# All low weight parts on VectorE, unscaled attention output, and diagonal blocks by the DMA's addressing, in a one-core hybrid encoder block

## The chip, the cores and the metric

The kernel runs on one core of one Trainium2 chip. A core has TensorE (PE, matmuls; its weight loads are shown apart as PEld), VectorE (DVE), ScalarE (ACT), GpSimd (POOL) and SyncE (SP, which here issues every DMA). Each engine works through its own instruction list in order; between engines there are only semaphores. The metric is the device time of one execution in microseconds. The kernel before takes 1120.7 us (median of 3 runs, 1119.09 to 1123.05).

## The reference

One layer of a streaming encoder for 512 tokens with 1024 features, in float32. Three sub-blocks follow each other, each with an RMS norm, a scale and a shift made from a conditioning vector, and a gated residual:

```
x = x + 0.5*g1 * swiglu(mod(x), ffn1)            # 1024 -> 2 x 2816 -> 1024
h = mod(x)
x = x + g2 * (concat(gated_delta_net(h), latent_attention(h)) @ w_out)
x = x + 0.5*g3 * swiglu(mod(x), ffn2)

# latent attention, per head of 4, per block of 128 queries
q_nope = rms(q_nope)*scale;  q_rope = rope(rms(q_rope))*scale
o_b = softmax(q k^T, chunk-causal) @ v
o_b = rms(o_b, mla_out_norm_w)                   # y * rsqrt(mean(y*y) + EPS)

# delta net, per head of 4: a triangular system per chunk of 64 tokens
M = I + strict_lower(beta * k k^T * decay);  W = solve(M, [beta*v, beta*exp(G)*k])
```

The norm after the softmax product is what the second part of the change uses: a row's scale cancels in it, up to the place of EPS.

## The kernel before

**Precision and weights.** Matmuls of float32 quality are made from three products of rounded parts (`mm3`, L261 to L263): high weight by high data, high by low, low by high. Each weight tile, a *unit* of 128 x 1024, is loaded by SP into `wr`; ACT casts it into the high part `wh` (L192), and the low part `wl = wr - wh` is one subtraction (L193). A switch `pool_lo` says which engine subtracts: VectorE in the two feed-forward blocks, GpSimd from the end of the first feed-forward block to the first units of the second one, that is in the mixer and the two norms around it. The tiles `wr`, `wh`, `wl` have four buffers each, so the load of a unit waits until the `wl` of the fourth unit before it is made, and its cast until PE has read the old one.

**The order of work.** A scheduler lays out each engine's list ahead of time from the program order and its own estimate of durations; the lists are then fixed. The program sets PE's order in some stretches (`matmuls_in_order`). The stages in the profiled time:

- 0 to about 380 us: modulation vectors and the first feed-forward block, mostly 128x512 matmuls.
- 380 to 430: the last output tiles of it, and `norm_half`: column sums of the squares `na` (L508), the row factor `ry` on GpSimd (L178), its diagonal `dg` (L428), a matmul that spreads it (L436) into `rb`, and then per feature tile `hm` (L454), `hh` (L456, ACT) and `hl` (L448), on which the next matmuls wait. It is done for each half of the tokens.
- 430 to about 500: latent projections (`latents`, `lifts`) and the first convolved tiles.
- 500 to 690: the dense units of the mixer are PE's filling, and between them run, as generators stepped in turn, `prep_q`, `prep_k`, `attend`, `delta_a`, `base_blocks`, `inverse`, `solve`.
- 690 to 760: the recurrence over 128-token blocks (`recur`, `gated_out`), the output projection (`out_half`, L1711) and the next `norm_half`.
- 760 to the end: the second feed-forward block.

**The places that the change touches.** `base_blocks` (L1172) inverts the 16x16 diagonal blocks of the triangular matrices `at`: it masks each `at` (L1182, four products on VectorE), folds the eight column groups by a reduction (L1184), writes the folded tile `bd` to DRAM and reads it back with a block on each partition (`ba`, L1186 and L1188), solves row by row on VectorE (L1200, L1201), and brings the result back in the same way (`t_d`, `t16`). `inverse` (L1211) starts from that result with four masked products per pair of chunks. `prep_q` (L1404) sums squares of queries by two reductions per tile, makes two row factors by integer start and three Newton steps (`rsqrt`, L173), and rotates the queries a block at a time (`rope`, L1490). `attend` (L1502) takes the row sum `l` of the exponentials, its reciprocal `li` on VectorE (L1519), and scales the product with it as it leaves PSUM (L1530, VectorE). `attended` (L1536) normalises the finished head. `z_done` in `mixer` (L1567) copies the gate projections out of PSUM on VectorE.

Of the kernel before, what the change touches and what calls it, by code (L numbers as in the profile page):

```python
# [77 lines left out]
class Block:  # L78
    def __init__(self, ctx, tc, ins, out):
# [111 lines left out]
    def split_w(self, raw, hi, lo):  # L191
        self.nc.scalar.copy(hi, raw)  # L192
        (self.nc.gpsimd if self.pool_lo else self.nc.vector).tensor_tensor(out=lo, in0=raw, in1=hi.bitcast(F32),  # L193
                                                                           op=ALU.subtract)
# [977 lines left out]
    def base_blocks(self):  # L1172

        nc, v = self.nc, self.nc.vector
        a_d = self.dp.tile([16, 8, 16, 16], F32, tag="a_d", name="a_d")
# [4 lines left out]
        m4 = self.dmask.unsqueeze(1).to_broadcast([P, 4, P])  # L1180
        for p in range(NB):
            m = self.slot(s="bm")  # L1182
            self.mul(m.rearrange("p (h c) -> p h c", h=4), self.at[p].rearrange("p (h c) -> p h c", h=4), m4)
            v.tensor_reduce(out=d[:, 64 * p:64 * p + 64].rearrange("p (h c) -> p h c", h=4),  # L1184
                            in_=m.rearrange("p (h i c) -> p h c i", h=4, i=8), axis=AX.X, op=ALU.add)
# [566 lines left out]
```

## Time and profile before

| | before |
|---|---|
| median of 3 runs | 1120.7 us |
| the profiled execution's own time | 1120.38 us |
| its span, first to last instruction | 1118.7 us |
| mean granted TensorE clock | 0.978 |
| PE busy | 1074.4 us, 96% |
| VectorE busy | 588.7 us, 53%, 1062 instructions |
| ACT busy | 376.4 us, 34%, 605 instructions |
| GpSimd busy | 132.6 us, 12%, 133 instructions |
| low weight parts on VectorE / on GpSimd | 133 / 37 |

Line numbers (L193) are those of the kernel before. Groups and waits carry the program's tile names, output first. The granted clock is a share of full speed: at 0.5 the same matmul takes twice the time, and PE is busy all the same, so a stage can lose time both as idle time of PE and as clock.

### The profile page before, as it was taken

To read this page: it belongs to the slowest core of one execution; us is meant where nothing else is said; L and a number is where in the kernel's file an instruction comes from. 1 tells how busy PE (TensorE), PEld (TensorE's weight loads), DVE (VectorE), ACT (ScalarE), POOL (GpSimd) and SP (SyncE) were. 2 spreads that over 40 slices of the span, in tenths; PEclk is the share of its full clock that TensorE was granted. 3 is DMA by queue.
4 is the path that set the end of the run, shared out by engine and by line. 5 is a ranking of instruction groups with operands and counts; after the bars stand their busy time and mean duration, and the time that the engine had idled before them with its cause. 6 is when DMAs were issued, how large, how long until landed. Compare 5 with 4: busy or idle time off the path is not lost. (4 is left out here: it accounts for less than half of the span.)

```text
span 1118.7 us, 14192 instructions
## 1 busy us (share of the span) xinstructions
PE 1074.4 (96%) x5591; PEld 891.8 (80%) x5591; DVE 588.7 (53%) x1062; ACT 376.4 (34%) x605; POOL 132.6 (12%) x133
## 2 busy tenths in 40 slices
PE   6999999999999979987999999979999999999998
PEld 5788788788887978966777768978888888888888
DVE  4489784333776266277777735875333333332220
ACT  4342322222222236464445244434232222222220
POOL 1000000000000245333122123440000000000000
PEclk8999999999999989998999989989999999999999
DMA  9989863333876363221112001123333333333420
GB/s 282 261 259 315 262 188 94 95 94 104 273 235 215 92 174 87 57 57 52 43 43 71 20 20 39 38 76 93 96 95 94 95 95 99 98 90 103 114 71 29
DMA packets 208625, 131.91 MB, mean 118 GB/s; under 512 B 11553, under 2 KB 192686, under 8 KB 208558
## 3 DMA queue, kind: packets, MB, share of 16 engines
q1 hardware_dynamic: 208558, 131.00, 39.6%
q8 instruction: 44, 0.72, 0.3%
q14 instruction: 23, 0.19, 0.1%
HBM read 128.63 MB, written 2.36 MB: 117 GB/s over the span
## 5 line engine op out<-in xcount | busy, mean ns | idle before, releaser
L261 PE MATMUL pa<-hh,wh 128*128 128x512 f32 (+1 forms) x885 | 341.5, 386 | 5.6 <-DVE xT L1711 2.4
L192 ACT CAST wh<-wr 128x1024 fp32r<-128x1024 f32 (+1 forms) x170 | 173.4, 1021 | 503.9 <-PE pa L262 322.6
L263 PE MATMUL pa<-hh,wl 128*128 128x512 f32 (+1 forms) x885 | 338.5, 382 | 0.0
L262 PE MATMUL pa<-hl,wh 128*128 128x512 f32 (+1 forms) x885 | 338.4, 382 | 0.1
L193 DVE TENSOR_TENSOR wl<-wr,wh 128x1024 fp32r<-128x1024 f32 (+1 forms) x133 | 156.6, 1178 | 208.5 <-ACT wh L192 199.9
L261 PEld LDWEIGHTS pa<-hh,wh 128*128 128x128 f32 x885 | 169.3, 191 | 40.7 <-issue 3.1
L263 PEld LDWEIGHTS pa<-hh,wl 128*128 128x128 f32 x885 | 169.1, 191 | 31.9 <-issue 0.5
L262 PEld LDWEIGHTS pa<-hl,wh 128*128 128x128 f32 x885 | 169.1, 191 | 30.7 <-issue 0.5
L261 PE MATMUL pa<-ah,wh 128*128 128x512 f32 (+1 forms) x418 | 150.1, 359 | 0.0
L263 PE MATMUL pa<-ah,wl 128*128 128x512 f32 (+1 forms) x418 | 148.8, 356 | 0.0
L262 PE MATMUL pa<-al,wh 128*128 128x512 f32 (+1 forms) x418 | 148.6, 356 | 0.0
L193 POOL TENSOR_TENSOR wl<-wr,wh 128x1024 fp32r<-128x1024 f32 (+1 forms) x37 | 89.5, 2426 | 274.8 <-ACT wh L192 243.7
L261 PEld LDWEIGHTS pa<-ah,wh 128*128 128x128 f32 x418 | 79.0, 189 | 12.7 <-ACT wh L192 1.7
L263 PEld LDWEIGHTS pa<-ah,wl 128*128 128x128 f32 x418 | 79.0, 189 | 11.3
L262 PEld LDWEIGHTS pa<-al,wh 128*128 128x128 f32 x418 | 79.0, 189 | 11.0
L592 DVE TENSOR_TENSOR af<-sg,pa 128x512 f32<-128x512 f32 x40 | 27.5, 687 | 104.7 <-PE pa L263 104.7
L546 DVE SCALAR_TENSOR_TENSOR aa<-ar,sc,aa 128x512 f32<-128x512 f32 x98 | 73.0, 749 | 10.5 <-DMA ar<-in_w_ada 8.8
L654 DVE SCALAR_TENSOR_TENSOR xT<-pa,mod,xT 128x512 f32<-128x512 f32 (+1 forms) x19 | 12.6, 666 | 50.3 <-PE pa L263 50.3
L1092 DVE SCALAR_TENSOR_TENSOR cv<-pa,cwT,cv 128x511 f32<-128x511 f32 (+2 forms) x36 | 26.5, 738 | 23.8 <-ACT cv L1090 23.5
L261 PE MATMUL pa<-mh,wh 128*128 128x256 f32 (+1 forms) x96 | 32.5, 343 | 0.0
L262 PE MATMUL pa<-ml,wh 128*128 128x256 f32 (+1 forms) x96 | 31.8, 333 | 0.0
L263 PE MATMUL pa<-mh,wl 128*128 128x256 f32 (+1 forms) x96 | 31.5, 330 | 0.0
(347 smaller groups left out, 1090.0 us busy)
## 6 DMA issues: line engine op xcount, KB each, us to landing
wr<-in_ffn_w_in SPq DMA_DIRECT2D x82, 512.0 KB, 3.8
ar<-in_w_ada SPq DMA_DIRECT2D x48, 512.0 KB, 5.8
wr<-in_ffn_w_out SPq DMA_DIRECT2D x34, 512.0 KB, 5.0
ar<-in_w_ada SPq DMA_DIRECT2D x48, 256.0 KB, 4.6
wr<-in_w_in SPq DMA_DIRECT2D x21, 512.0 KB, 3.6
wr<-in_ffn_w_out SPq DMA_DIRECT2D x17, 384.0 KB, 3.5
wr<-in_w_out SPq DMA_DIRECT2D x8, 512.0 KB, 3.4
wr<-in_ffn_w_in SPq DMA_DIRECT2D x8, 384.0 KB, 7.2
```

What stands on the lines that cost most here:

```text
L192: self.nc.scalar.copy(hi, raw)
L193: (self.nc.gpsimd if self.pool_lo else self.nc.vector).tensor_tensor(out=lo, in0=raw, in1=hi.bitcast(F32), op=ALU.subtract)
L261: mm(out, wh, xh, start=start, stop=False)
L262: mm(out, wh, xl, start=False, stop=False)
L263: mm(out, wl, xh, start=False, stop=stop)
L546: nc.vector.scalar_tensor_tensor(out=acc, in0=a, scalar=sc, in1=acc, op0=ALU.mult, op1=ALU.add)
L592: nc.vector.tensor_tensor(out=a, in0=s, in1=pu, op=ALU.mult)
L654: nc.vector.scalar_tensor_tensor(out=self.xT[t][:, ts], in0=p[:, ts], scalar=gate[:, t:t + 1], in1=self.xT[t][:, ts], op0=ALU.mult, op1=AL ...
L1092: nc.vector.scalar_tensor_tensor(out=a[:, d:], in0=p[:, :NT - d], scalar=wj(3 - d), in1=a[:, d:], op0=ALU.mult, op1=ALU.add)
```

## The change

`pool_lo` goes: every low weight part is made on VectorE. `attend` keeps the row sums of a head in a tile `al`, drops the reciprocal, and ACT copies the unscaled product; `attended` puts EPS times the square of the sum into the norm in place of EPS, which gives the same value. In `base_blocks` ACT copies the 32x32 diagonal squares of `at` (16 copies), and the two reads from DRAM pick the 16x16 blocks by their addresses. `prep_q` sums squares by one reduction per tile, makes both row factors as one tile of 32 columns, and rotates two blocks at a time. `inverse` makes its start in one product. `z_done` copies on ACT.

```
     def split_w(self, raw, hi, lo):
         self.nc.scalar.copy(hi, raw)
-        (self.nc.gpsimd if self.pool_lo else self.nc.vector).tensor_tensor(out=lo, in0=raw, in1=hi.bitcast(F32),
-                                                                           op=ALU.subtract)
+        self.nc.vector.tensor_tensor(out=lo, in0=raw, in1=hi.bitcast(F32), op=ALU.subtract)
...
-        a_d = self.dp.tile([16, 8, 16, 16], F32, tag="a_d", name="a_d")
+        a_d = self.dp.tile([16, 4, 32, 32], F32, tag="a_d", name="a_d")
...
         for p in range(NB):
-            m = self.slot(s="bm")
-            self.mul(m.rearrange("p (h c) -> p h c", h=4), self.at[p].rearrange("p (h c) -> p h c", h=4), m4)
-            v.tensor_reduce(out=d[:, 64 * p:64 * p + 64].rearrange("p (h c) -> p h c", h=4),
-                            in_=m.rearrange("p (h i c) -> p h c i", h=4, i=8), axis=AX.X, op=ALU.add)
-        nc.sync.dma_start(by_token(a_d), d.rearrange("p (q c) -> p q c", q=16))
+            for j in range(4):
+                js = slice(32 * j, 32 * j + 32)
+                nc.scalar.copy(d[js, p * P:(p + 1) * P].rearrange("p (h c) -> p h c", h=4),
+                               self.at[p][js, :].rearrange("p (h c) -> p h c", h=4)[:, :, js])
+        nc.sync.dma_start(a_d.rearrange("q j s c -> (j s) q c"), d.rearrange("p (q c) -> p q c", q=16))
         a = self.slot(s="ba")[:, :256]
-        nc.sync.dma_start(a, by_block(a_d))
+        for e in range(2):
+            es = slice(16 * e, 16 * e + 16)
+            nc.sync.dma_start(a[64 * e:64 * e + 64, :].rearrange("p (s c) -> p s c", s=16),
+                              a_d.rearrange("q j s c -> (q j) s c")[:, es, es])
...
-        nc.sync.dma_start(by_block(t_d), tt)
+        for e in range(2):
+            nc.sync.dma_start(t_d.rearrange("q (j e) s c -> e (q j) (s c)", e=2)[e], tt[64 * e:64 * e + 64, :])
...
-        for h in range(4):
-            self.mul(t[:, hs(h)].rearrange("p (i c) -> p i c", i=8),
-                     self.t16[:, 4 * p + h:4 * p + h + 1, :].to_broadcast([P, 8, 16]),
-                     self.dmask.rearrange("p (i c) -> p i c", i=8))
+        self.mul(t.rearrange("p (h i c) -> p h i c", h=4, i=8),
+                 self.t16[:, 4 * p:4 * p + 4, :].unsqueeze(2).to_broadcast([P, 4, 8, 16]),
+                 self.dmask.rearrange("p (i c) -> p i c", i=8).unsqueeze(1).to_broadcast([P, 4, 8, 16]))
...
-                sv = s[:, :384].rearrange("p (h d) -> p h d", h=2)
-                nc.vector.tensor_reduce(out=sq_n[:, c], in_=sv[:, :, :128], axis=AX.X, op=ALU.add)
-                nc.vector.tensor_reduce(out=sq_r[:, c], in_=sv[:, :, 128:], axis=AX.X, op=ALU.add)
+                nc.vector.tensor_reduce(out=s3[:, c:c + 6], in_=s[:, :384].rearrange("p (e d) -> p e d", e=6), axis=AX.X,
+                                        op=ALU.add)
...
-        rqn, rqr = self.rms_cols(sq_n, 16, 128), self.rms_cols(sq_r, 16, 64)
+        s3 = s3.rearrange("p (q e) -> p q e", e=3)
+        nc.vector.tensor_tensor(out=ve[:, :16], in0=s3[:, :, 0], in1=s3[:, :, 1], op=ALU.add)
...
+        r = self.rsqrt(ve, 32, room[:, 80:112], room[:, 112:144])
...
-        m, l, li = self.small(1, "mx"), self.small(1, "l"), self.small(1, "li")
+        m = self.small(1, "mx")
...
-        self.table(pr[:, :n], ps[:, :n], AF.Exp, bias=m, accum_out=l)
-        nc.vector.reciprocal(out=li, in_=l)
+        self.table(pr[:, :n], ps[:, :n], AF.Exp, bias=m, accum_out=self.al[h][:, i:i + 1])
...
-        nc.vector.tensor_scalar(out=self.ao[h][:, ts], in0=po[:, :P], scalar1=li, scalar2=None, op0=ALU.mult)
+        nc.scalar.copy(self.ao[h][:, ts], po[:, :P])
...
-        ss = self.small(4, "as")
+        ss, ve = self.small(4, "as"), self.small(4, "ve")
+        nc.vector.scalar_tensor_tensor(out=ve, in0=self.al[h], scalar=EPS, in1=self.al[h], op0=ALU.mult, op1=ALU.mult)
         self.head_squares(self.ao[h], ss)
-        r = self.rms_cols(ss, 4, P)
+        nc.vector.scalar_tensor_tensor(out=ve, in0=ss, scalar=1.0 / P, in1=ve, op0=ALU.mult, op1=ALU.add)
+        r = self.rsqrt(ve, 4)
...
         def z_done(i, p):
             z = self.slot(s="z")
-            nc.vector.tensor_copy(z, p)
+            nc.scalar.copy(z, p)
```

The scheduler lays the lists out anew, so more moves than the diff tells. Three places matter below; in the lists of the change a line number is one or two lower than before.

First, VectorE in `norm_half` of the first tokens, at the end of the first feed-forward block (`xT` is the residual's update, `na` the sum of squares). Before, from the update of the last tile but one half to the column sum's factor `ve`:

```order
L448 SCALAR_TENSOR_TENSOR hl_3164<-hm_3315,mod_1297,hh_3163 128x256
L448 SCALAR_TENSOR_TENSOR hl_3166<-hm_3318,mod_1297,hh_3165 128x256
L454 SCALAR_TENSOR_TENSOR hm_3323<-xT_106,mod_1791,rb_3238 128x256
L454 SCALAR_TENSOR_TENSOR hm_3326<-xT_106,mod_1791,rb_3238 128x256
L448 SCALAR_TENSOR_TENSOR hl_3168<-hm_3323,mod_1297,hh_3167 128x256
L448 SCALAR_TENSOR_TENSOR hl_3170<-hm_3326,mod_1297,hh_3169 128x256
L654 SCALAR_TENSOR_TENSOR xT_106<-pa_3290,mod_1297,xT_106 128x256
L472 TENSOR_TENSOR na_2257<-na_2257,sq_3392 128x256
L514 TENSOR_SCALAR ve_3442<-pb_3439 128x2
```

The same place in the change:

```order
L192 TENSOR_TENSOR wl_3387<-wr_3385,wh_3386 128x1024
L446 SCALAR_TENSOR_TENSOR hl_3164<-hm_3315,mod_1297,hh_3163 128x256
L446 SCALAR_TENSOR_TENSOR hl_3166<-hm_3318,mod_1297,hh_3165 128x256
L452 SCALAR_TENSOR_TENSOR hm_3323<-xT_106,mod_1791,rb_3238 128x256
L652 SCALAR_TENSOR_TENSOR xT_106<-pa_3290,mod_1297,xT_106 128x256
L452 SCALAR_TENSOR_TENSOR hm_3326<-xT_106,mod_1791,rb_3238 128x256
L192 TENSOR_TENSOR wl_3538<-wr_3536,wh_3537 128x1024
L446 SCALAR_TENSOR_TENSOR hl_3168<-hm_3323,mod_1297,hh_3167 128x256
L446 SCALAR_TENSOR_TENSOR hl_3170<-hm_3326,mod_1297,hh_3169 128x256
L470 TENSOR_TENSOR na_2257<-na_2257,sq_3392 128x256
L512 TENSOR_SCALAR ve_3442<-pb_3439 128x2
```

Two low weight parts have come in, and the update `xT` has moved ahead of the last `hm` and the last two `hl`.

Second, VectorE in the norm at the mixer's end, from the row factor on. Before:

```order
L514 TENSOR_SCALAR ve_6465<-pb_6462 128x2
L428 TENSOR_SCALAR dg_6469<-ident_92,ry_6467 128x128 x2
L472 TENSOR_TENSOR na_5662<-na_5662,sq_6459 128x256
L1711 SCALAR_TENSOR_TENSOR xT_106<-pa_6478,mod_1791,xT_106 128x256
L472 TENSOR_TENSOR na_5662<-na_5662,sq_6492 128x256
L454 SCALAR_TENSOR_TENSOR hm_6499<-xT_106,mod_2754,rb_6497 128x256
```

In the change:

```order
L512 TENSOR_SCALAR ve_6378<-pb_6375 128x2
L426 TENSOR_SCALAR dg_6382<-ident_92,ry_6380 128x128 x2
L192 TENSOR_TENSOR wl_6387<-wr_6385,wh_6386 128x1024
L470 TENSOR_TENSOR na_5584<-na_5584,sq_6372 128x256
L1718 SCALAR_TENSOR_TENSOR xT_106<-pa_6391,mod_1791,xT_106 128x256
L1718 SCALAR_TENSOR_TENSOR xT_106<-pa_6420,mod_1791,xT_106 128x256
L192 TENSOR_TENSOR wl_6439<-wr_6437,wh_6438 128x1024
L470 TENSOR_TENSOR na_5584<-na_5584,sq_6405 128x256
L452 SCALAR_TENSOR_TENSOR hm_6412<-xT_106,mod_2754,rb_6410 128x256
```

Two low weight parts now stand between the diagonal and the first `hm`.

Third, SP's queue around the blocks of `base_blocks`, in the change (`x2` is two DMAs):

```order
L1180 DMA a_d<-bd_4858 128x16x32
L116 DMA wr_5627<-in_w_out 128x4x256
L1184 DMA ba_4876<-a_d 64x16x16 x2
L116 DMA wr_5752<-in_w_out 128x4x256
L116 DMA wr_5908<-in_w_out 128x4x256
L1202 DMA t_d<-bt_4879 64x256 x2
L116 DMA wr_6029<-in_w_out 128x4x256
L1204 DMA t_5112<-t_d 128x16x16
```

Before, `ba` followed `a_d` at once, and one weight load stood between `ba` and `t_d`; now it is one and two.

More of the change, by code (lines that the diff above doesn't have):

```diff
@@ L170, in table, with rsqrt @@
         self.tabled = ins.name
-    def rsqrt(self, v, n):
+    def rsqrt(self, v, n, y=None, t=None):
         nc = self.nc
-        y = self.small(n, "ry", bufs=6)
+        y = self.small(n, "ry", bufs=6) if y is None else y
         if n <= 8:
@@ L179, in rsqrt @@
             return y
-        t = self.small(n, "rt")
+        t = self.small(n, "rt") if t is None else t
         nc.vector.tensor_scalar(out=t.bitcast(I32), in0=v.bitcast(I32), scalar1=1, scalar2=None,
@@ L1203, in base_blocks @@
                 yield
-        nc.sync.dma_start(by_block(t_d), tt)
+        for e in range(2):
+            nc.sync.dma_start(t_d.rearrange("q (j e) s c -> e (q j) (s c)", e=2)[e], tt[64 * e:64 * e + 64, :])
         self.t16 = self.slot(s="t16")[:, :256].rearrange("p (q c) -> p q c", q=16)
-        nc.sync.dma_start(self.t16, by_token(t_d))
+        nc.sync.dma_start(self.t16, t_d.rearrange("q i s c -> (i s) q c"))
         yield
@@ L1416, in prep_q @@
             if b % 2:
                 yield
-        rqn, rqr = self.rms_cols(sq_n, 16, 128), self.rms_cols(sq_r, 16, 64)
-        qr = []
-        for b in range(NB):
-            x = self.slot(s="qrx")
-            xv = x[:, :256].rearrange("p (h c) -> p h c", h=4)
-            for g in range(2):
-                qv = q[b][g][:, :384].rearrange("p (h d) -> p h d", h=2)[:, :, 128:]
-                self.mul(xv[:, 2 * g:2 * g + 2, :], qv, self.bc(rqr[:, 4 * b + 2 * g:4 * b + 2 * g + 2], 2, 64))
+        s3 = s3.rearrange("p (q e) -> p q e", e=3)
@@ new lines, in prep_q @@
+        nc.vector.tensor_tensor(out=ve[:, :16], in0=s3[:, :, 0], in1=s3[:, :, 1], op=ALU.add)
+        nc.vector.tensor_scalar(out=ve[:, :16], in0=ve[:, :16], scalar1=1.0 / 128, scalar2=EPS, op0=ALU.mult, op1=ALU.add)
+        nc.vector.tensor_scalar(out=ve[:, 16:], in0=s3[:, :, 2], scalar1=1.0 / 64, scalar2=EPS, op0=ALU.mult, op1=ALU.add)
+        r = self.rsqrt(ve, 32, room[:, 80:112], room[:, 112:144])
+        rqn, rqr = r[:, :16], r[:, 16:]
+        qr = []
+        for b in range(0, NB, 2):
+            x = self.slot(s="qrx").rearrange("p (b h c) -> p b h c", b=2, h=4)
+            for e in range(2):
+                for g in range(2):
+                    qv = q[b + e][g][:, :384].rearrange("p (h d) -> p h d", h=2)[:, :, 128:]
+                    c = 4 * (b + e) + 2 * g
+                    self.mul(x[:, e, 2 * g:2 * g + 2, :], qv, self.bc(rqr[:, c:c + 2], 2, 64))
@@ L1509, in attend @@
             self.ao[h] = self.slot(s="ao")
+            self.al[h] = self.const([P, NB], s="al")
         ps = self.aux()
```

32 lines of the change are left out of this document (13 added, 19 removed).

## The prediction

> **What bounds the kernel now.** I read the engine summary and the shares of the chain that ended last first.
>
> ```profile
> PE 1074.4 (96%) x5591; PEld 891.8 (80%) x5591; DVE 588.7 (53%) x1062; ACT 376.4 (34%) x605; POOL 132.6 (12%) x133
> PE 37%; DVE 2%; issue 1%; ACT 0%; POOL 0%; POOLq 0%; ACTq 0%
> ```
>
> PE is the bound, VectorE is half idle, GpSimd almost idle. The change takes nothing off PE, so it can only win PE's idle time and the clock. Next, the busy time by stage. The columns after the stretch and its length are PE, PEld, DVE, ACT and POOL busy with instruction counts, then granted clock, DMA share and GB/s.
>
> ```profile
> 0.00:380.00 380.00, 371.22 (x1780) 299.65 (x1781) 225.73 (x364) 113.86 (x158) 6.20 (x51) 0.99 0.67 202
> 380.00:500.00 120.00, 112.53 (x670) 101.22 (x669) 64.72 (x138) 58.28 (x104) 47.41 (x27) 0.97 0.33 92
> 500.00:780.00 280.00, 255.75 (x1590) 211.22 (x1591) 195.72 (x453) 119.34 (x236) 79.02 (x57) 0.94 0.17 49
> 780.00:1118.70 338.70, 334.89 (x1554) 279.66 (x1552) 102.52 (x109) 84.94 (x107) 0.00 (x0) 1.00 0.31 91
> ```
>
> GpSimd works only where the change is made, 380 to 780 us, and there stands nearly all that can be won: PE idles 120 - 112.5 + 280 - 255.75 = 31.7 us, and the missing clock is worth about 0.03 x 120 + 0.06 x 280 = 20.4 us. The change touches neither of the outer stages except through the list, and they are tight at full clock. Then, PE's waits in 380 to 780 us: in total, times, longest.
>
> ```profile
> PE pb L508 <- DVE na L472: 7.2, 2, 5.2
> PE pb L1100 <- ACT cv L167: 5.1, 1, 5.1
> PE pb L1471 <- DVE kn L886: 4.4, 1, 4.4
> PE pb L436 <- DVE dg L428: 3.0, 2, 2.2
> PE pa L261 <- DVE xT L1711: 2.4, 1, 2.4
> PE pa L261 <- DVE cv L1092: 1.8, 1, 1.8
> PE pa L261 <- DVE z L1568: 1.3, 1, 1.3
> ```
>
> These nine waits are 25.2 of the 31.7 us, and all but one name VectorE, although it is busy only 65% of these stages (64.7 + 195.7 of 400). The timeline of the longest shows why: start, duration, engine, instruction, and in brackets the wait before it.
>
> ```profile
> 407.03 4.83 POOL L193 TENSOR_TENSOR wl<-wr,wh 128x1024 fp32r<-128x1024 f32 x2 [2.10 <-ACT wh L192]
> 407.39 2.26 DVE L448 SCALAR_TENSOR_TENSOR hl<-hm,mod,hh 128x256 fp32r<-128x256 f32 x1 [0.86 <-ACT hh L456]
> 409.58 0.47 DVE L654 SCALAR_TENSOR_TENSOR xT<-pa,mod,xT 128x256 f32<-128x256 f32 x1
> 410.09 0.42 ACT L470 ACTIVATE sq<-xT 128x256 f32<-128x256 f32 x1 [1.79 <-DVE xT L654]
> 410.54 1.60 DVE L472 TENSOR_TENSOR na<-na,sq 128x256 f32<-128x256 f32 x1 [0.48 <-ACT sq L470]
> 412.29 0.99 PE L508 MATMUL pb<-ones,na 128*128 128x1 f32 x4 [5.19 <-DVE na L472]
> ```
>
> GpSimd makes two `wl` from 407.03 to 411.86. `hl` starts inside the first and takes 2.26 us, `na` starts inside the second and ends with it; `xT` between them, which reads PSUM, is not held. The usual duration of such an instruction shows that it was held, not slow (minimum, median, maximum in ns over the whole run, then the mean in 380 to 780 us):
>
> ```profile
> L454 DVE SCALAR_TENSOR_TENSOR hm<-xT,mod,rb x32: 470/478/2603, 394.2 to 761.4; 128x256 f32<-128x256 f32 x32
> L448 DVE SCALAR_TENSOR_TENSOR hl<-hm,mod,hh x32: 467/480/2505, 395.9 to 762.4; 128x256 fp32r<-128x256 f32 x32
> L428 DVE TENSOR_SCALAR dg<-ident,ry x12: 274/283/2408, 14.1 to 753.0; 128x128 f32<-128x128 f32 x12
> L454 DVE SCALAR_TENSOR_TENSOR hm<-xT,mod,rb 128x256 f32<-128x256 f32 x32 | 21.6, 691 | 8.3 <-ACT rb L438 8.3
> L448 DVE SCALAR_TENSOR_TENSOR hl<-hm,mod,hh 128x256 fp32r<-128x256 f32 x32 | 20.5, 655 | 2.3 <-ACT hh L456 2.2
> L428 DVE TENSOR_SCALAR dg<-ident,ry 128x128 f32<-128x128 f32 x8 | 6.1, 808 | 2.5 <-POOL ry L178 2.5
> ```
>
> Median against mean: 32 x 0.213 + 32 x 0.175 + 8 x 0.525 = 16.6 us of VectorE's busy time in three groups is holding. Last, the clock behind such gaps.
>
> ```profile
> 410.00:420.00 10.00, 7.71 (x45) 7.69 (x46) 3.41 (x8) 1.38 (x4) 2.56 (x2) 0.66 0.99 316
> 580.00:590.00 10.00, 8.16 (x36) 6.74 (x36) 9.75 (x16) 2.77 (x6) 5.16 (x4) 0.89 0.42 99
> 650.00:660.00 10.00, 9.09 (x63) 6.74 (x64) 3.93 (x11) 5.59 (x10) 0.00 (x0) 0.63 0.00 0
> ```
>
> Behind the 5.2 us wait 3.4 us of clock are lost, behind the 1.8 us wait in 580 to 590 still 1.1. In 650 to 660 the clock is low though GpSimd is idle: I take that for another thing, and its 3.7 us for staying. So 20.4 - 3.7 = 16.7 us of clock hang on the gaps, 0.66 us for each us of the nine waits.
>
> **The change, part by part.** *The low weight parts.* What they take on either engine:
>
> ```profile
> L193 POOL TENSOR_TENSOR wl<-wr,wh x37: 1837/2397/2966, 379.3 to 746.6; 128x1024 fp32r<-128x1024 f32 x36, 128x768 fp32r<-128x768 f32 x1
> L193 DVE TENSOR_TENSOR wl<-wr,wh x133: 951/1225/1229, 27.6 to 1094.1; 128x1024 fp32r<-128x1024 f32 x110, 128x768 fp32r<-128x768 f32 x23
> ```
>
> VectorE gets 37 x 1.225 = 45.3 us, GpSimd loses about 37 x 2.4 = 89 us. An instruction that comes to VectorE at any moment met a GpSimd `wl` in 89/400 = 22% of cases, and was held for up to 2.4 us; it will meet one of its own engine in 45/400 = 11%, for 0.6 us in the mean, 0.07 us each where `hm` loses 0.21 now. About two thirds of the excess should go.
>
> *What VectorE sheds.* Rows of 380 to 780 us:
>
> ```profile
> L1530 DVE TENSOR_SCALAR ao<-pb,li 128x128 f32<-128x128 f32 x16 | 5.5, 346 | 6.6 <-PE pb L1529 6.5
> L886 DVE TENSOR_TENSOR bm<-at,mk 128x512 f32<-128x512 f32 x4 | 4.5, 1136 | 0.0
> L1184 DVE TENSOR_REDUCE bd<-bm 128x64 f32<-128x512 f32 x4 | 4.1, 1034 | 0.0
> L1568 DVE COPY z<-pa 128x512 f32<-128x512 f32 x4 | 2.7, 675 | 0.0
> L1519 DVE RECIPROCAL li<-l 128x1 f32<-128x1 f32 x16 | 2.5, 157 | 2.4 <-ACT pr L167 2.3
> ```
>
> 5.5 + 4.5 + 4.1 + 2.7 + 2.5 = 19.3 us. The two small additions to each head's norm and the fused sums, row factors and rotations of `prep_q` roughly halve a few dozen short instructions; I count them as nothing, since PE has dense units as filling there (bounds 0 and 3 us off VectorE). With 16.6 us of holding gone in three groups alone, VectorE's load there goes from 260 to about 260 + 45.3 - 19.3 - 16.6 = 270 us of 400: nearly even.
>
> *What ACT gets.* 16 unscaled copies, 4 copies of `z` and 16 block copies. The nearest rows, a small copy on ACT that appears below at 0.26 us and the 0.675 us of `z` on VectorE as an upper bound, give 32 x 0.26 + 4 x 0.675 = 11 us on an engine with 119.3 of 280 busy. That is cover enough; without it the `ao` copies, which PE's next product of the head awaits, would cost 16 x 0.26 = 4 us at most. Estimate 0.
>
> *The diagonal blocks.* The products and reductions on VectorE, (4.5 + 4.1) = 8.6 us one after another, become 16 copies on ACT, and there are two more DMAs in SP's queue.
>
> ```profile
> L1250 ACT COPY Y<-pb 32x128 f32<-32x128 f32 x8 | 2.1, 258 | 3.4 <-PE pb L1248 3.3
> a_d<-bd SPq DMA_DIRECT2D x1, 128.0 KB, 3.3
> ```
>
> 16 x 0.258 = 4.1 us replace 8.6; the reads by short pieces may take as long as this write by short pieces, 3.3 us, and weight loads now stand ahead of `ba` and `t_d` in SP's queue. At best the chain is 4.5 us shorter, at worst a few us longer; PE's list has dense units there and none of the nine waits is the solve's, so 0, with -2 and +3 as bounds. In a sentence of its own: the Trainium skill ("DMA: Bandwidth & Descriptors") says that descriptors below 512 bytes lose much of the rate, and the new read's 64-byte pieces would fall under it; at 128 KB the row of 3.3 us bounds what it can mean here.
>
> *The nine waits, one by one.* Ahead of `cv` on VectorE stands a held mask product:
>
> ```profile
> 580.52 2.50 DVE L886 TENSOR_TENSOR bm<-at,mk 128x512 f32<-128x512 f32 x1
> ```
>
> The products of this kind go, so `cv`: 1.8 to 0; `z`, on ACT now: 1.3 to 0. `na`: `hl` at 0.48 for 2.26 and `na` by about 1.2 shorter take 3.0 off the long one, 1.2 off the short one, 7.2 to 3. `cv` on ACT and `kn` end chains of several held instructions: I leave 1.5 of 5.1 and 1 of 4.4. `dg`: mean 0.81 to 0.28, 3.0 to 1. `xT`: 2.4 to 1. Saved: 4.2 + 3.6 + 3.4 + 2.0 + 1.4 + 1.8 + 1.3 = 17.7 us. The bounds are 0 and 25.2.
>
> *What the change adds as a wait.* VectorE's list is in order, so each `wl` in it stands until ACT has cast its unit, and the cast stands until PE has let go of the tile. What that comes to now, on ACT:
>
> ```profile
> ACT wh L192 <- PE pa L262: 29.1, 13, 4.5
> ```
>
> Behind a `wl` on VectorE stand, in the two places shown, the last `hl` and `na` (first norm), and the first `hm` (last norm); PE waits for each. The scheduler puts a `wl` where it believes the cast done; I charge four places with one `wl` each, 4 x 1.225 = 4.9 us; the bounds are 0 and all 29.1.
>
> *What can still hold VectorE.* GpSimd keeps `upo`, `kbg`, `kd`, `Sg` and the shares of `na`:
>
> ```profile
> L886 POOL TENSOR_TENSOR upo<-upo,ry 128x256 f32<-128x256 f32 x8 | 4.9, 650 | 1.5 <-DVE ry L188 1.5
> ```
>
> At 0.65 us each they hold little. Beside it: the Trainium skill ("SBUF — State Buffer", section "Who interferes with whom") makes the port pair that VectorE and GpSimd share an exclusive lock. The timeline of 407 us agrees (`hl` and `na` end with a `wl`). By that rule a `wl` on VectorE, which has two SBUF inputs, becomes itself something that is held and that GpSimd's remaining work waits for; by the 0.65 us of the row above that is a few us on either engine, and the sum would be the same.
>
> *Sum.* Idle: 17.7 - 4.9 = 12.8 us less. Clock: 0.66 x 12.8 = 8.5 us less. The profiled execution goes from 1118.7 to 1118.7 - 21.3 = 1097.4 us of span. Its own time was 1120.38, 1.7 above its span, and the median of the runs 0.3 above that: I add 2.0 and get **1099.4 us**.
>
> **Rivals.** *(a) VectorE's own `wl` takes the place of GpSimd's.* The lists put a `wl` right ahead of the awaited instructions at two of the places. If each of the nine waits keeps one, 9 x 1.225 = 11.0 us come off the saving, 6.7 us of idle time are won, and with gaps still near 1.8 us the clock is not: 1120.7 - 6.7 = 1114 us. For it: the lists. Against it: a `wl` on VectorE is half as long as GpSimd's, and VectorE is idle a third of the time in these stages, so that most of the 37 can stand elsewhere.
>
> *(b) All gaps fall below what the clock answers to.* Then the whole 16.7 us of clock come back and no `wl` costs: 17.7 + 16.7 = 34.4, 1086 us. For it: the low clock in these stages follows gaps, save at 650. Against it: a gap of only 1.8 us already cost clock. Beside it: the Trainium skill ("TensorE: Matmul & The Clock Gate", on the clock gate) has PE throttled after an idle window of some 3.4 us, by which nearly all dips would go with the long gaps; the row of 580 to 590 does not agree.
>
> *(c) Slower: VectorE stands at a `wl` whose cast is late.* One mechanism: the 29.1 us that ACT's casts wait for PE now pass to VectorE, which cannot run past them, and what PE needs stands behind. It decides once more than 17.7 us of the 29.1 reach PE. At three quarters, 21.8 us, PE's idle time grows by 4.1 and the clock by 0.66 x 4.1 = 2.7: 1127.5 us. For it: the casts wait 13 times, up to 4.5 us. Against it: in the feed-forward blocks 133 `wl` stand in VectorE's list in the same way, and PE is idle for only 338.7 - 334.9 = 3.8 us of the last of these stages.
>
> *(d) The change does not do what it says:* that VectorE's holding has another cause than GpSimd's `wl`. Then VectorE just gets 26 us more work where PE waits for it, and the time is that of (a) or (c).
>
> **How the numbers follow.** The forecast, 1099 us, with its own range of 1090 to 1108 (the unknown terms: waits saved 13 to 22 instead of 17.7, new waits 0 to 8, blocks -2 to +3): 0.60. (a) with (d), 1114: 0.19. (b), 1086: 0.12. (c), 1127: 0.09. To leave out no more than 2 in 10 the range has to hold most of (a) and half of (b): 1085 to 1117 us. A measurement of this kernel tells from no change about 0.3%, 3.4 us, so faster is below 1117.3: the forecast, (b) and three quarters of (a), 0.60 + 0.12 + 0.14 = 0.86. The rest of (a), 0.05, is no change, and (c), 0.09, slower.
>
> **What would show it.** In the changed profile `hm`, `hl` and `dg` should have means near their medians (0.48, 0.48, 0.28 us) in 380 to 780 us; PE's waits for `na`, `kn` and `cv` should be below 2 us each, and the clock of 500 to 780 us should rise from 0.94 to 0.96 or 0.97, with 650 to 660 still low. VectorE should be busy some 270 us of these 400, and ACT 11 us more than now. Rival (a) shows as waits on the same instructions with a `wl` just ahead on VectorE. (c) shows as idle time of VectorE ahead of `wl`, ended by ACT's `wh`, with PE waiting for VectorE. The block chain is right if PE's wait on the product behind `t16` stays below 1 us. The prediction is wrong if the means fall as told and PE's waits do not: then what PE waited for was due at that time anyway, by another chain. It is wrong in another way if the outer stages lose their tightness through the new lists.

## The result and the profile after

| | before | after |
|---|---|---|
| median | 1120.8 us | 1094.2 us (1090.9 to 1095.4) |
| ratio, 95% interval | | 0.9753 (0.973 to 0.9776) |
| span of the profiled execution | 1118.7 us | 1089.2 us |
| PE busy, 5591 matmuls in both | 1074.4 us | 1063.4 us |
| PE idle (span minus busy) | 44.3 us | 25.8 us |
| mean granted clock | 0.978 | 0.993 |

The change takes 26.7 us off the median, where 21.3 were forecast; the time lies in the range. In the profiled executions 29.5 us go: 18.5 us of PE's idle time, and 11.0 us of PE's busy time, which for the same matmuls is clock. That profile is of the fastest of the four executions (1090.9 us; the others had a clock of 0.988 to 0.990 for 0.993), so it shows some 3 us more than the median does.

The engine summary of the page after:

```profile
PE 1063.4 (98%) x5591; PEld 882.4 (81%) x5591; DVE 571.3 (52%) x1021; ACT 387.1 (36%) x641; POOL 45.7 (4%) x96
```

The stretch of 380 to 780 us as one row, in the columns of the prediction, first of the kernel before:

```profile
380.00:780.00 400.00, 368.27 (x2260) 312.44 (x2260) 260.44 (x590) 177.62 (x340) 126.43 (x83) 0.95 0.22 62
```

and after:

```profile
380.00:780.00 400.00, 387.02 (x2378) 327.26 (x2377) 252.11 (x559) 196.07 (x386) 38.73 (x45) 0.98 0.24 68
```

PE does 118 matmuls more in these 400 us, at a higher clock, and its idle time there falls from 31.7 to 13.0 us. VectorE, which got 37 subtractions of 1.2 us, is busy *less* than before. The groups of VectorE that were held, after, in the same stretch:

```profile
L192 DVE TENSOR_TENSOR wl<-wr,wh 128x1024 fp32r<-128x1024 f32 x45 | 54.9, 1221 | 42.1 <-ACT wh L191 41.4
L452 DVE SCALAR_TENSOR_TENSOR hm<-xT,mod,rb 128x256 f32<-128x256 f32 x32 | 14.7, 478 | 4.1 <-ACT rb L436 4.1
L446 DVE SCALAR_TENSOR_TENSOR hl<-hm,mod,hh 128x256 fp32r<-128x256 f32 x32 | 14.7, 478 | 0.5 <-ACT hh L454 0.5
L426 DVE TENSOR_SCALAR dg<-ident,ry 128x128 f32<-128x128 f32 x8 | 1.9, 283 | 2.5 <-POOL ry L177 2.5
```

Means of 478, 478 and 283 ns stand where 691, 655 and 808 stood: the holding is gone from them. And PE's waits after:

```profile
PE pb L1554 <- DVE on L882: 3.2, 3, 1.5
PE pb L1439 <- DVE qro L1505: 3.2, 2, 2.6
PE pa L260 <- DVE hl L446: 2.9, 4, 1.4
PE pa L259 <- ACT z L1575: 0.8, 1, 0.8
PE pb L1475 <- DVE kro L1471: 0.7, 1, 0.7
PE pb L506 <- DVE na L470: 0.6, 2, 0.3
PE pb L1367 <- DVE on L882: 0.5, 2, 0.4
...
PE pa L259 <- DVE xT L1718: 0.3, 1, 0.3
```

Of the nine waits of the prediction (25.2 us) `na`, `xT` and `z` are left with 1.7 us together, and `kro`, in the place of `kn`, with 0.7. New are `qro` (0.3 before) and `hl` (none before); the waits for `on` are 3.7 us for 3.8 before.

### The profile page after: what moved, and what is told of

Same layout as the page of the kernel before. It is cut to its first block, busy times and chain, and to the rows that moved or that the text cites. A ratio compares the mean times of both kernels' runs of the same rounds, so it can differ in the third digit from the quotient of the medians.

```text
span 1089.2 us, 14151 instructions
## 1 busy us (share of the span) xinstructions
PE 1063.4 (98%) x5591; PEld 882.4 (81%) x5591; DVE 571.3 (52%) x1021; ACT 387.1 (36%) x641; POOL 45.7 (4%) x96
## 4 chain that ended last, share of the span: by engine, by line
PE 86%; DVE 6%; ACT 3%; issue 2%; DMA 2%; POOL 1%; SPq 0%; DVEq 0%; POOLq 0%; ACTq 0%
PE pa L259 25%; PE pa L260 25%; PE pa L261 25%; DVE wl L192 1%; PE pb L1518 1%; POOL ry L177 1%; PE pb L1517 1%; PE pb L259 1%; PE pb L260 1%; PE pb L261 1%; PE pb L1534 1%; PE pb L1144 1%; PE pb L407 1%; DMA vb<-in_gdn_a_log 1%; DVE hl L446 1%
## 5 line engine op out<-in xcount | busy, mean ns | idle before, releaser
L191 ACT CAST wh<-wr 128x1024 fp32r<-128x1024 f32 (+1 forms) x170 | 173.3, 1021 | 506.0 <-PE pa L260 344.8
L192 DVE TENSOR_TENSOR wl<-wr,wh 128x1024 fp32r<-128x1024 f32 (+1 forms) x170 | 201.3, 1185 | 232.5 <-ACT wh L191 226.2
L259 PEld LDWEIGHTS pa<-hh,wh 128*128 128x128 f32 x885 | 166.5, 188 | 37.1 <-issue 3.8
L260 PEld LDWEIGHTS pa<-hl,wh 128*128 128x128 f32 x885 | 166.6, 188 | 34.7 <-DVE hl L446 4.6
L261 PEld LDWEIGHTS pa<-hh,wl 128*128 128x128 f32 x885 | 166.5, 188 | 32.1 <-issue 1.2
L592 ACT CAST ah<-af 128x512 fp32r<-128x512 f32 x44 | 27.4, 622 | 10.3 <-DVE af L590 10.3
L593 DVE TENSOR_TENSOR al<-af,ah 128x512 fp32r<-128x512 f32 x44 | 30.1, 685 | 0.8 <-ACT ah L592 0.7
```

What stands on the lines that cost most here:

```text
L192: self.nc.vector.tensor_tensor(out=lo, in0=raw, in1=hi.bitcast(F32), op=ALU.subtract)
L259: mm(out, wh, xh, start=start, stop=False)
L260: mm(out, wh, xl, start=False, stop=False)
L261: mm(out, wl, xh, start=False, stop=stop)
L592: nc.scalar.copy(ah, a)
L593: nc.vector.tensor_tensor(out=al, in0=a, in1=ah.bitcast(F32), op=ALU.subtract)
```

## The experiments

Two things had to be told apart. The **theory** is holding: GpSimd's subtractions, which read two SBUF operands, stop VectorE's instructions, and taking them away is the gain. The **rival** is load: VectorE was relieved of some 20 us by the other parts, and that is the gain; a weaker form of it is that the lists were merely laid out better. All times are medians, beside runs of the kernel before on the same chip (1120.5 to 1120.9 us); numbers in brackets are 95% intervals of the ratio.

### The low weight parts alone

```
-        (self.nc.gpsimd if self.pool_lo else self.nc.vector).tensor_tensor(out=lo, in0=raw, in1=hi.bitcast(F32), op=ALU.subtract)
+        self.nc.vector.tensor_tensor(out=lo, in0=raw, in1=hi.bitcast(F32), op=ALU.subtract)
```

> The kernel before with one edit: every low weight part on VectorE. Theory (holding: the gain is that GpSimd's subtractions no longer hold VectorE's instructions): hm and hl in 380 to 780 us go from means of 0.69 and 0.66 us to below 0.50 us, and most of the gain of 26.7 us comes from this edit alone: 1094 to 1105 us. Rival (load: the gain comes from what VectorE sheds in the other parts, which make room for the 45 us): VectorE gets 45 us more and sheds nothing, so PE's waits for VectorE stay or grow, 1112 us or more.

Measured: 1103.2 us, 0.9833 (0.9803 to 0.9864): 17.3 of the 26.7 us. The stretch of 380 to 780 us and the two groups there:

```profile
380.00:780.00 400.00, 381.94 (x2323) 323.36 (x2323) 264.76 (x632) 182.41 (x346) 39.88 (x46) 0.96 0.23 65
L453 DVE SCALAR_TENSOR_TENSOR hm<-xT,mod,rb 128x256 f32<-128x256 f32 x32 | 14.7, 478 | 5.6 <-ACT rb L437 5.6
L447 DVE SCALAR_TENSOR_TENSOR hl<-hm,mod,hh 128x256 fp32r<-128x256 f32 x32 | 14.7, 479 | 0.5 <-ACT hh L455 0.5
```

VectorE got 45.3 us of work, shed nothing, and is busy 264.8 us for 260.4. So about 45.3 - 4.3 = 41 us of its busy time before was holding (an estimate, since the same 400 us hold a little more of the program; over the whole span, 588.9 us busy beside 588.7, it comes to 45). PE's idle time falls from 44.3 to 31.9 us, 12.4 of the 18.5 us. Load speaks against a gain here, and there is one.

### Everything but the low weight parts

```
-        self.nc.vector.tensor_tensor(out=lo, in0=raw, in1=hi.bitcast(F32), op=ALU.subtract)
+        (self.nc.gpsimd if self.pool_lo else self.nc.vector).tensor_tensor(out=lo, in0=raw, in1=hi.bitcast(F32), op=ALU.subtract)
```

(in the changed kernel, with the places that set `pool_lo`).

> The changed kernel with one part undone: the low weight parts of the mixer are back on GpSimd. Theory (holding): hm and hl have means above 0.62 us again, PE waits for VectorE as before, 1110 to 1122 us. Rival (load): VectorE has shed its 19 us and did not get the 45, so the gain stays or grows, 1100 us or less.

Measured: 1124.1 us, 1.0058 (1.0029 to 1.0086), slower than before, and 2 us above what the theory expected. `hl` and `hm` have means of 655 and 624 ns again. PE's waits:

```profile
PE pb L1558 <- DVE on L886: 6.3, 3, 2.9
PE pb L508 <- DVE na L472: 5.7, 2, 5.2
PE pb L1100 <- ACT cv L167: 5.5, 1, 5.5
```

The waits of before are back (`on` is longer) though VectorE has shed its work. By itself, what was shed is worth nothing while GpSimd holds the rest.

### GpSimd reads again, or only writes

In the changed kernel GpSimd gets something to do behind each of VectorE's 37 low parts; the output is that of the change. First it repeats the subtraction into the raw tile, which nobody reads any longer:

```
         self.nc.vector.tensor_tensor(out=lo, in0=raw, in1=hi.bitcast(F32), op=ALU.subtract)
+        if self.pool_lo:
+            self.nc.gpsimd.tensor_tensor(out=raw, in0=raw, in1=hi.bitcast(F32), op=ALU.subtract)
```

> The changed kernel, and behind each low weight part of the mixer GpSimd makes the same subtraction once more, into the raw tile that nobody reads any longer. VectorE's list is nearly that of the change. Theory (holding by GpSimd's reading): hm and hl have means above 0.60 us again though VectorE's work is that of the change, PE's waits for VectorE return, 1105 to 1125 us. Rivals (load, or the new order of the lists): as the change, 1091 to 1097 us.

Measured: 1133.2 us, 1.0108 (1.0085 to 1.0132), 39 us above the change and 8 above the range expected. VectorE's list differs from the change's in 38 of 1021 places. The timeline of the first norm, and the groups in 380 to 780 us:

```profile
399.09 2.58 POOL L195 TENSOR_TENSOR wr<-wr,wh 128x1024 f32<-128x1024 f32 x1 [2.28 <-DVE wl L193]
399.33 3.01 DVE L455 SCALAR_TENSOR_TENSOR hm<-xT,mod,rb 128x256 f32<-128x256 f32 x2
```

```profile
L449 DVE SCALAR_TENSOR_TENSOR hl<-hm,mod,hh 128x256 fp32r<-128x256 f32 x32 | 23.0, 738 | 0.5 <-ACT hh L457 0.5
L455 DVE SCALAR_TENSOR_TENSOR hm<-xT,mod,rb 128x256 f32<-128x256 f32 x32 | 22.6, 724 | 7.0 <-ACT rb L439 7.0
```

Two `hm`, 0.96 us otherwise, take 3.01: the first starts under GpSimd's subtraction and ends only 0.3 us behind it, the second follows at its usual length. The means are above those of before. Second, it fills the same tile with zeros, twice:

```
+        if self.pool_lo:
+            for _ in range(2):
+                self.nc.gpsimd.memset(raw, 0.0)
```

> The changed kernel, and behind each low weight part of the mixer GpSimd fills the raw tile, which nobody reads any longer, with zeros, twice: it is busy about as long as with a subtraction and lets go of the tile as late, but reads nothing. All lists but GpSimd's are those of the change, save some loads in SP's. The Trainium skill (SBUF — State Buffer, Who interferes with whom) says that a VectorE instruction with two SBUF inputs contends with a GpSimd instruction that reads SBUF, not with one that only writes. By holding through reads: hm and hl stay below 0.50 us and the time at 1091 to 1098 us; only dg, an instruction with one tensor input, may be held. Rival (any long GpSimd instruction holds VectorE, or the late release of the raw tile costs): as the run in which GpSimd subtracts again, 1105 us or more.

Measured: 1095.5 us, 0.9773 (0.9734 to 0.9812): the time of the change. The stretch, the same two groups, and the same place in the norm:

```profile
380.00:780.00 400.00, 385.18 (x2347) 326.99 (x2346) 250.31 (x555) 193.77 (x383) 108.24 (x120) 0.97 0.24 67
L456 DVE SCALAR_TENSOR_TENSOR hm<-xT,mod,rb 128x256 f32<-128x256 f32 x32 | 14.7, 479 | 7.7 <-ACT rb L440 7.7
L450 DVE SCALAR_TENSOR_TENSOR hl<-hm,mod,hh 128x256 fp32r<-128x256 f32 x32 | 14.7, 478 | 0.5 <-ACT hh L458 0.5
```

```profile
402.38 0.87 DVE L450 SCALAR_TENSOR_TENSOR hl<-hm,mod,hh 128x256 fp32r<-128x256 f32 x2
402.52 1.96 POOL L196 MEMSET wr<- 128x1024 f32 x2 [0.55 <-DVE wl L193]
403.18 0.48 DVE L456 SCALAR_TENSOR_TENSOR hm<-xT,mod,rb 128x256 f32<-128x256 f32 x1
```

GpSimd is busy 108 us here, against 39 in the change, and lets go of the tile late as before; `hl` and `hm` run under its fills (0.95 us each) at their usual 0.48 us. The lists of PE, VectorE and ACT are the change's own in this kernel. So neither a busy GpSimd nor late tiles cost this kernel anything that the medians show, and the layout of the lists is not the gain: the end of GpSimd's reading is. The Trainium skill ("SBUF — State Buffer", "Who interferes with whom") states just this for instructions with two SBUF inputs; the two runs agree, 724 ns against 479.

### The other parts, one at a time, in the kernel before

Attention and `z` (with `al` in `attended`'s norm, as in the change, of which the diff shows two lines):

```
-        nc.vector.tensor_scalar(out=self.ao[h][:, ts], in0=po[:, :P], scalar1=li, scalar2=None, op0=ALU.mult)
+        nc.scalar.copy(self.ao[h][:, ts], po[:, :P])
...
-            nc.vector.tensor_copy(z, p)
+            nc.scalar.copy(z, p)
```

> The kernel before with one part of the change: unscaled attention output copied by ACT, no reciprocal, and z copied by ACT. Theory (holding): VectorE sheds 10.7 us, which PE waited for in one place only (z, 1.3 us); holding stays: 1115 to 1121 us. Rival (load): a third of the gain or more, 1112 us or less.

Diagonal blocks (`base_blocks` of the change; the diff leaves out its DMAs):

```
-            self.mul(m.rearrange("p (h c) -> p h c", h=4), self.at[p].rearrange("p (h c) -> p h c", h=4), m4)
-            v.tensor_reduce(...)
+            for j in range(4):
+                nc.scalar.copy(d[js, ...], self.at[p][js, :]...[:, :, js])
```

> The kernel before with one part of the change: the diagonal blocks by ACT's copies and by the addresses of the two reads. Theory: VectorE sheds 8.6 us, one wait of 1.8 us behind a held mask product goes, and the clock dip behind it (1.7 us): 1116 to 1121 us; PE's wait on the product behind t16 stays below 1 us. Rival (load): 1113 us or less. Rival (the reads by 64-byte pieces are slow): the wait on the product behind t16 grows by some us, above 1121 us.

Queries and the start of the inversion (`prep_q`, `rope`, `rsqrt`, `inverse` of the change; the diff shows the sums of squares):

```
-                nc.vector.tensor_reduce(out=sq_n[:, c], in_=sv[:, :, :128], axis=AX.X, op=ALU.add)
-                nc.vector.tensor_reduce(out=sq_r[:, c], in_=sv[:, :, 128:], axis=AX.X, op=ALU.add)
+                nc.vector.tensor_reduce(out=s3[:, c:c + 6], in_=s[:, :384].rearrange("p (e d) -> p e d", e=6), axis=AX.X, op=ALU.add)
```

> The kernel before with one part of the change: one reduction a tile, one tile of row factors and rotations two blocks at a time in the preparation of the queries, and one product at the start of the inversion. Theory: the short instructions that were held up to 2.4 us each become fewer, the longest waits of this place (cv 5.1, kn 4.4 us) may shrink by a third, 1112 to 1121 us. Rival (load): 1110 us or less.

| in the kernel before | median | ratio (interval) | PE idle in its profile |
|---|---|---|---|
| attention and `z` | 1114.4 us | 0.9943 (0.9923 to 0.9964) | 44.6 us |
| diagonal blocks | 1124.2 us | 1.003 (1.0019 to 1.0042) | 49.3 us |
| queries, inversion | 1114.6 us | 0.9958 (0.9935 to 0.9981) | 45.4 us |

Beside 44.3 us of idle time before, none of the three wins any in its profile. What attention and queries win in the median (6.3 us, which lies between the two expectations, and 6.1) goes with the clock: the ten runs of attention alone go from 1112.2 us at a granted clock of 0.988 to 1123.0 us at 0.977 (the profiled one), where the kernel before has 0.978 in its profile. The three do not add up either: their medians make a gain of 9 us together, but the run of everything but the low weight parts, which has all three, is 3.6 us slower than before. The blocks' own loss, 3 us above what its theory expected, shows in PE's waits:

```profile
PE pb L1548 <- DVE on L886: 5.2, 3, 2.9
```

`na` is as before (7.2 us), and the new wait is on `on`, the scaled head output (1.6 us before), which stands elsewhere in VectorE's list; no wait names the solve. In none of the three runs does PE wait for one of the new copies or the reads, and for the start of the inversion (`t`) at most 1.4 us.

### What is left on GpSimd

In the changed kernel the products `kbg`, `kd`, `Sg` and `upo` and GpSimd's share of the sums `na` go to VectorE; of the four products the diff shows one.

```
-        self.mul(h4(kbg), h4(kt), self.bc(self.eG[:, c4], 4), nc.gpsimd)
+        self.mul(h4(kbg), h4(kt), self.bc(self.eG[:, c4], 4))
...
-        eng = nc.gpsimd if w < NT and ts.start == 0 else nc.vector
+        eng = nc.vector
```

> The changed kernel, with the products kbg, kd, Sg and upo and GpSimd's share of the sums of squares on VectorE too, so that only the small row factors stay on GpSimd. Theory (holding): what is left of holding is small; 23 us less on GpSimd put some 13 us on VectorE, half of it where PE has filling: 1091 to 1098 us, no change that can be told. Rival (VectorE now close to its limit): 1099 us or more. Rival (the remaining reads hold as the low parts did): 1090 us or less.

Measured: 1084.0 us, 0.9684 (0.9653 to 0.9714): 10 us better than the change, and the best of all kernels here. The theory had expected no gain, and I had counted these products at nothing; the rival, that the remaining reads hold too, came true. Their place is the longest wait that the change has left; its timeline, in the change:

```profile
488.45 5.62 POOL L882 TENSOR_TENSOR upo<-upo,sq 128x256 f32<-128x256 f32 x8 [23.91 <-DVE sq L187]
488.92 2.15 DVE L882 TENSOR_TENSOR qrx<-upo,sq 128x128 f32<-128x128 f32 x4
...
494.67 0.66 PE L1439 MATMUL pb<-ident,qro 128*128 128x128 f32 x4 [2.58 <-DVE qro L1505]
495.13 0.88 DVE L882 TENSOR_TENSOR qrx<-upo,sq 128x128 f32<-128x128 f32 x4
```

Eight `upo` in a row slow VectorE for 5.6 us: four `qrx` take 2.15 us beside them and 0.88 us after them, and the rotation behind them (`rt`, `qro`) 3.55 us for 2.13; together that is 2.7 us, about PE's wait. With these products on VectorE that wait is in no list any more, and the stretch reads:

```profile
380.00:780.00 400.00, 390.81 (x2425) 330.01 (x2424) 262.51 (x590) 199.22 (x390) 16.96 (x19) 1.00 0.25 71
```

The longest waits left there are 1.5 us (`on`) and 1.4 us (`hl`). Between the two profiles, though, only 1.5 of 8.7 us are idle time of PE (25.8 to 24.3); the other 7.2 are its busy time, that is clock (0.993 to 1.000). So most of this gain came by the clock, which the last section comes back to.

To see which of the two edits does it, the four products alone, of which the diff shows `upo`:

```
-        self.mul(qv, qv, self.bc(rqn[:, 4 * b + 2 * g:4 * b + 2 * g + 2], 2), nc.gpsimd)
+        self.mul(qv, qv, self.bc(rqn[:, 4 * b + 2 * g:4 * b + 2 * g + 2], 2))
```

> The changed kernel with kbg, kd, Sg and upo on VectorE, GpSimd keeping its share of the sums of squares. If the products' reads hold VectorE at the queries (a wait of 2.6 us on qro with held instructions ahead of it), nearly all of the 10 us that the run with both had is here: 1084 to 1088 us. If the sums of squares do it: 1091 to 1095 us.

Measured: 1086.3 us, 0.9696 (0.9664 to 0.9729). The products, then; the 2.3 us that the sums add are within the spread of the two (1082.0 to 1088.2 and 1083.4 to 1090.8).

And both edits, products and sums, in the kernel before, where the low weight parts stay on GpSimd:

```
-        self.mul(h4(kbg), h4(kt), self.bc(self.eG[:, c4], 4), nc.gpsimd)
+        self.mul(h4(kbg), h4(kt), self.bc(self.eG[:, c4], 4))
...
-        eng = nc.gpsimd if w < NT and ts.start == 0 else nc.vector
+        eng = nc.vector
```

> The kernel before with only the rest of GpSimd's work (kbg, kd, Sg, upo, its share of na) on VectorE; the low weight parts stay on GpSimd. Theory (the low parts' reads hold whatever is on VectorE): more instructions on VectorE meet the 37 subtractions: no gain, 1117 to 1128 us. Rival (the products and sums are what holds): 1110 us or less.

Measured: 1114.2 us, 0.9942 (0.9923 to 0.996), between the two expectations. PE's idle time is 46.6 us, not less than before; its profile has a clock of 0.988. So here too PE won no idle time. `hm` and `hl` have means of 624 and 655 ns: the low weight parts hold them whatever else VectorE does.

### The other parts, where little is left to hold

The kernel before, with the low weight parts and the rest of GpSimd's work on VectorE and no other part of the change (the diff leaves out the four products):

```
-        (self.nc.gpsimd if self.pool_lo else self.nc.vector).tensor_tensor(out=lo, in0=raw, in1=hi.bitcast(F32), op=ALU.subtract)
+        self.nc.vector.tensor_tensor(out=lo, in0=raw, in1=hi.bitcast(F32), op=ALU.subtract)
...
-        eng = nc.gpsimd if w < NT and ts.start == 0 else nc.vector
+        eng = nc.vector
```

> The kernel before with the low weight parts and the rest of GpSimd's work on VectorE (only the small row factors stay), and no other part of the change. Theory (holding, and VectorE's load matters little): the three other parts are worth 3 to 9 us, so 1086 to 1094 us. Rival (load matters once nothing holds VectorE): 1097 us or more.

Measured: 1097.5 us, 0.9792 (0.9756 to 0.9828). Against 1084.0 us the three other parts are worth 13.6 us here, more than the 3 to 9 I expected, so in this surrounding the rival, load, has a point. In the profiles, which are 16.1 us apart, only 3.2 us are idle time of PE (27.5 for 24.3); the rest is its busy time, that is clock (0.985 for 1.000). From the run of the low weight parts alone to the change the same three parts take off 6.1 us of idle time (31.9 to 25.8). The two longest of PE's waits:

```profile
PE pb L1231 <- DVE t L885: 4.6, 1, 4.6
PE pb L1545 <- DVE on L885: 3.5, 2, 2.8
```

The wait for `t`, the start of the inversion, is 4.6 us in the run of the low weight parts alone too, and in neither list of the change and of the best kernel. Which of the three parts takes it away (one product in place of four, or what stood ahead of it on VectorE) was not tried apart.

Last, the best kernel with `base_blocks` of the kernel before:

```
-            for j in range(4):
-                nc.scalar.copy(d[js, ...], self.at[p][js, :]...[:, :, js])
+            self.mul(m.rearrange("p (h c) -> p h c", h=4), self.at[p].rearrange("p (h c) -> p h c", h=4), m4)
+            v.tensor_reduce(...)
```

> The kernel of the run that put the rest of GpSimd's work on VectorE too (1084 us), with the diagonal blocks made as before (masked products and reductions on VectorE). Alone, this part of the change made the kernel 3.4 us slower. If the blocks cost something by themselves (two more DMAs, copies on ACT): 1079 to 1082 us. If they only moved the lists and the phase of the clock: 1082 to 1090 us.

Measured: 1088.9 us, 0.9711 (0.9692 to 0.973), 5.0 us slower than with the new blocks. The same edit that costs 3.4 us in the kernel before gains 5 here, and not by idle time: PE idles 22.7 us with the old blocks and 24.3 with the new. It is clock, 0.989 for 1.000. With the old blocks PE waits 2.6 us for `on`, and the clock is at half behind it:

```profile
597.30:607.50 10.20, 9.36 (x25) 6.16 (x24) 3.21 (x6) 2.37 (x6) 0.00 (x0) 0.50 0.10 34
```

So the edit has no price of its own that the runs show; it moves the lists, and with them where `on` falls.

## Why the prediction was right

**What bounds the kernel** and **the mechanism** were right, and shown: taking GpSimd's subtractions away gives 17.3 of the 26.7 us by itself, putting the reads back takes all of the gain, and putting writes in their place takes nothing.

**The holding's size was the term mis-sized.** The prediction summed three groups to 16.6 us and forecast VectorE at 270 us of the 400; it is 252.1. By the run of the low weight parts alone some 41 us were held. The rest sat in some twenty other groups, none with more than 2.7 us above its own minimum, which the costliest lines of a table do not show; the step to take was to count what VectorE would be busy with without the excess in every group, not in the three that PE waits for.

**The nine waits.** Saved were to be 17.7 of 25.2 us. By the list after, 25.2 - 1.7 = 23.5 went, or 22.8 with `kro` in the place of `kn`. I left 7.5 us for chains of several held instructions (`na` 3, `cv` 1.5, `kn` 1, `dg` 1, `xT` 1); where every member of a chain was held, nearly the whole wait went.

**The new waits** were charged at 4.9 us; `hl` with 2.9 and `qro` with 2.9 more than before make 5.8. Of `hl`'s waits two, of 1.39 and 0.56 us, stand behind a `wl`. The first came just as the lists said, a `wl` ahead of the last two `hl` (the timeline after):

```profile
403.35 1.22 DVE L192 TENSOR_TENSOR wl<-wr,wh 128x1024 fp32r<-128x1024 f32 x1
404.49 0.87 DVE L446 SCALAR_TENSOR_TENSOR hl<-hm,mod,hh 128x256 fp32r<-128x256 f32 x2
405.02 0.39 PE L260 MATMUL pa<-hl,wh 128*128 128x256 f32 x1 [1.39 <-DVE hl L446]
```

The other, `qro`, was not a `wl` at all but GpSimd's `upo`, of which the prediction said that they hold little. That sentence was wrong: 0.65 us each, but eight in a row. That it did not upset the sum was luck: it was about as large as the waits behind a `wl` that did not come.

**The clock** gave 11.0 us for 18.5 us of idle time in these profiles, 0.59 us for each, where 0.66 was used. By the median, if its idle time is that of the profile, it gave 26.7 - 18.5 = 8.2 us (an estimate), where 8.5 were forecast. A fixed price for each us of idle time is a rough summary (last section). I took the low clock at 650 us for something of its own that stays. In the change it does, at 640:

```profile
640.00:650.00 10.00, 10.00 (x74) 8.51 (x74) 2.42 (x5) 2.11 (x7) 4.21 (x5) 0.51 0.00 0
```

but it need not: in the kernel without GpSimd's products and sums the same stage runs at full clock:

```profile
640.00:650.00 10.00, 10.00 (x98) 9.17 (x96) 8.21 (x14) 4.05 (x7) 0.00 (x0) 1.00 0.01 2
```

PE's wait on `on` just ahead is 1.5 us in the first and 0.7 in the second; whether that wait decides it is open.

**ACT's share** was sized right, and its price was near nothing: these rows, after, make 11.2 us for the 11 forecast, and PE waits 0.8 us for `z`, none for `ao`.

```profile
L1178 ACT COPY bd<-at 32x128 f32<-32x128 f32 x16 | 4.7, 295 | 0.2
L1535 ACT COPY ao<-pb 128x128 f32<-128x128 f32 x16 | 4.1, 268 | 8.5 <-PE pb L1534 8.3
L1575 ACT COPY z<-pa 128x512 f32<-128x512 f32 x4 | 2.4, 589 | 0.0
```

**The diagonal blocks.** Before, from the write's issue to the first product of the solve:

```profile
584.25 0.37 SPq L1186 DMA_DIRECT2D a_d<-bd  x1
...
589.90 0.15 DVE L886 TENSOR_TENSOR bw<-ba,bt 128x1 f32<-128x1 f32 x1
```

and after:

```profile
552.87 4.90 ACT L1178 COPY bd<-at 32x128 f32<-32x128 f32 x16
557.79 0.37 SPq L1180 DMA_DIRECT2D a_d<-bd  x1
...
565.15 0.16 DVE L882 TENSOR_TENSOR bw<-ba,bt 128x1 f32<-128x1 f32 x1 [0.75 <-DMA ba<-a_d]
```

The stretch of DMAs takes 7.4 us for 5.7, 1.7 more, and the copies take 4.9 us where VectorE took 9.6 (574.7 to 584.2). The whole is 3.0 us shorter, between the 4.5 us shorter and the few us longer of the prediction. The two reads by short pieces (64 KB each) landed in 2.8 us, below the row of 3.3 us, and PE does not wait for it: 0, as forecast.

**The rivals.** (a), VectorE's own `wl` in the place of GpSimd's, came true at two places, with 1.4 and 0.6 us. (b) would have needed full clock; the change had 0.98 in 380 to 780 us, the kernel without the products and sums 1.00. (c) had its condition, but not its effect: VectorE stands at a `wl` for ACT's cast for 41.4 us in 380 to 780, more than the 29.1 us of ACT's own wait before, and still none of PE's waits for VectorE follows such a late `wl` within 3 us. What stands behind one was not due yet. (d) fell with the low weight parts alone, which brought the means of `hm` and `hl` to 478 and 479 ns.

## What to carry to other kernels

An idle engine is not free help. GpSimd's subtractions took 89 us that PE hardly waited for, and held VectorE for some 41 us; moving them alone won 17.3 of the change's 26.7 us. The sign in a profile is a group whose mean is far above its median, with ends that fall on the other engine's ends. Work that only wrote cost nothing on it that the medians show; work that read, even eight products of 0.65 us in a row, was better off on the engine that it held. And edits that shed load from an engine may show little until the thing that holds that engine is gone: with the low weight parts on GpSimd the three other parts gave no idle time back, alone (44.6, 49.3 and 45.4 us) or together (47.6) beside 44.3, and with the low weight parts moved they took it from 31.9 to 25.8. Compare idle time and clock apart: a median mixes them, and the medians of the three did not add up.
